# MoBA scores of the decoded samples on VectorE in place of TensorE, with their key pages spread over the attention stage

## The chip, the cores and the metric

The kernel runs on one core of a Trainium2 chip. A core has a matrix engine (TensorE, PE in the profile; its weight loads have a row of their own, PEld), a vector engine (VectorE, DVE), a scalar engine (ScalarE, ACT), a general one (GpSimd, POOL) and a queue that issues most transfers (SyncE, SP). Each runs its own list of instructions in order, and they wait for one another by semaphores. The metric is the time of one execution on the device in microseconds (us), as the median of several runs. About 0.3% (some 1.8 us) is what a measurement of this kernel can tell from no change.

## The reference, cut to what matters

One decoder layer is run for a prompt of 512 tokens and for 8 decoded samples of one token each. Two token mixers work side by side on the same input: a sparse attention with three branches (NSA), and MoBA, 8 heads of 64 channels over blocks of 256 keys. Each sample has 1024 past keys, in 8 pages of 128 keys, which a page table finds in a cache. What the change touches is the product of a sample's MoBA query with all its past keys:

```python
# qc (8 samples, 1, 8 heads, 64); kb: past keys by block of 256; kmean: mean key of each block
gs  = einsum('bqhd,bnhd->bqhn', qc, kmean)             # which 3 blocks count
sel = top_k(where(block < own, gs, -inf), 3)
s   = einsum('bqhd,bhqkld->bhqkl', qc, ksel) * 0.125 + bias
p   = masked_softmax(concat([s, s_own]))
out = einsum('bhqn,bhqnd->bqhd', p, vsel) + ...
```

The kernel makes all 1024 products of a head and sample once (64 rows of 1024 scores, with the mean score of a block for the choice), leaves out the blocks that weren't chosen, and multiplies by the values. Everything is in float32; the large products of the prompt take a float32 number apart into two parts of a faster format (high and remainder), and three matmuls on the parts make one product.

## The kernel before, in words

The weights come in 46 column blocks of 512 KB. A block is split into its two parts (high on ScalarE, remainder on VectorE or GpSimd by a written list, `HL_LO`, tile `hl`) and is multiplied with the input `hT` in 48 matmuls of 260 columns, into two banks `d`. These are the rows `d<-hTh,hl` and `d<-hTl,hl`, the bulk of the work. Between them run three other streams:

- **the compression** (`phi_pair`, `dec_cmp`; tiles `craw`, `u`, `pr`, `cvd`), in the first quarter;
- **the attention of the prompt** (`attend`, 24 jobs of 4 row blocks): scores into a bank `s` (`s<-kd,q`), bias and row minimum on VectorE (L1273, L1275), exponentials on ScalarE (L1278), a reciprocal on VectorE (L1279), the scaling on GpSimd (L1280), transposes into a bank `pt` (L355), a copy to SBUF (L1288, tiles `pp`), and the product with the values into a bank `o`;
- **the decoded samples** (`dec_a`, `dec_b`), which read pages through three buffers `cr` of 1 MB (tiles `raw`) and use the single bank `e`. Their order was: the pages `slck` and `wink` of NSA's keys, 16 tiles `mobk` of MoBA's keys, NSA's values, 16 tiles `mobv` of MoBA's values.

For MoBA's scores a key page lies with the channels on the 128 partitions. A tile `zm` holds each sample's query in a column of its own among zeros, and for each of the 16 tiles four matmuls of 512 columns (`e<-raw,zm`, 32 output rows each) add the page's scores into the bank, one quarter of the partitions for each pair of heads; after 8 tiles the bank is copied to half of `xm`.

What sets the order: `line_up` lays each engine's instructions out by a written table (`QUEUES`), and a second table (`SLOTS`) says which of its buffers a tile takes. No scheduler decides anything at run time; an instruction that waits holds up all that stand behind it on its engine. On SP a page load that waits for one of the three `cr` buffers holds up the weight loads behind it.

Of the kernel before, what the change touches and what calls it, by code (L numbers as in the profile page):

```python
# [18 lines left out]
T = 512  # L19
NS = 8  # L20
# [38 lines left out]
COPY_ENG = "daa"  # L59
# [15 lines left out]
for _name, _w in (("ident", 128), ("rowmask", 1), ("ones", 1), ("p16", 1),  # L75
# [20 lines left out]
    "kv.kl": "01",  # L96
# [14 lines left out]
    "de.cr": "01201201201201201201201202010120120120120120",  # L111
# [4 lines left out]
    "at.pp0": "012012012012012012012012",  # L116
# [6 lines left out]
    "fm.m": "0123456120",  # L123
# [13 lines left out]
702-704 659-664 705-710 677-682 750-755 690-695 756-761 720-722 539-541 711-719 542-550 723-743 768-785 762-767 786-797 804-815 798-803 816-821
829-840 883-894 841-846 895-900 847-849 901-906 919-924 683-685 850-852 907-912 859-861 686-687 913-918 688-689 950-955 862-870 956-961 925-930
871-873 853-858 874-876 822-824 877-879 931-936 880-882 825-826 944-949 962-967 827-828 974-979 968-973 980-1009 937-943 1022-1033 1040-1047 1034-1039
1048-1065 1010-1015 1072 1016-1021 1085 1066-1071 1073-1078 1110-1113 1092-1097 1079-1084 1126 1098-1103 1086-1091 1139 1104-1109 1120-1125 1114-1119  # L140
1225-1226 1211-1212 1133-1138 1127-1132 1146-1157 1140-1145 1174-1179 1241-1243 1170-1173 1233-1234 1158-1169 1180-1185 1187-1192 1255-1256 1244-1246
1186 1247-1248 1193-1198 1263-1264 1213-1218 1271-1272 1219-1224 1249-1254 1199-1210 1227-1232 1257-1262 1235-1240 1289-1290 1307-1308 1279-1288
1295-1300 1265-1270 1291-1294 1273-1278 1309-1314 1331-1332 1301-1302 1317-1318 1345-1350 1355-1360 1315-1316 1325-1330 1319-1324 1339-1344 1333-1338
1361-1362 1351-1354 1365-1370 1385-1390 1363-1364 1303-1306 1371-1374 1395-1402 1375-1376 1451-1456 1383-1384 1377-1382 1403-1408 1461-1466 1391-1394
1409-1410 1449-1450 1415-1420 1423-1428 1421-1422 1411-1414 1433-1438 1493-1498 1431-1432 1429-1430 1439-1444 1507-1512 1485-1490 1457-1460 1491-1492
1445-1448 1503-1506 1475-1478 1529-1534 1467-1468 1519-1520 1469-1474 1513-1518 1499-1502 1555-1560 1521-1526 1563-1568 1479-1484 1561-1562 1587-1592
1595-1600 1527-1528 1573-1578 1543-1554 1603-1608 1615-1616 1585-1586 1539-1542 1617-1622 1601-1602 1569-1572 1627-1632 1609-1614 1583-1584 1653-1658
1535-1538 1579-1582 1593-1594 1669-1674 1635-1640 1633-1634 1661-1666 1651-1652 1675-1680 1623-1626 1693-1696 1645-1650 1667-1668 1641-1644 1681-1688
1659-1660 1705-1710 1697-1704 1689-1692 1737-1744 1719-1722 1711-1718 1727-1732 1745-1750 1769-1770 1754-1755 1723-1726 1771-1776 1756-1761 1751-1752
1762-1767 1781-1786 1791-1792 1733-1736 1817-1822 1793-1798 1831-1836 1809-1811 1753 1803-1808 1823-1824 1768 1812-1814 1777-1780 1815-1816 1787-1790  # L150
1827-1830 1851-1854 1799-1802 1855-1856 1837-1842 1825-1826 1857-1862 1845-1850 1843-1844 1879-1884 1887-1892 1885-1886 1911-1916 1901-1906 1909-1910
1867-1878 1897-1900 1925-1928 1863-1866 1929-1930 1945-1950 1893-1896 1919-1924 1943-1944 1907-1908 1959-1964 1917-1918 1965-1968 1931-1936 1994-1999
# [192 lines left out]
def build(tc, A):  # L345
# [26 lines left out]
    with ExitStack() as es:  # L372
# [25 lines left out]
        def p_e():  # L398
            return bank("e", 1)
# [229 lines left out]
        def early_load(n):  # L629
# [4 lines left out]
            for hf in range(2):  # L634
                if n == "ks" and hf:
                    t = [kvp.tile([128, T], F32R, name="kl", tag="kl", bufs=2) for _ in range(2)]
# [1392 lines left out]
```

## Time and profile before

| | |
|---|---|
| median of 3 runs | 586.03 us (584.95 to 586.43) |
| the profiled execution | 584.64 us, its span 582.8 us |
| granted TensorE clock | 0.996 |
| moved by DMA | 124.83 MB, 214 GB/s on the mean |

The span is the time from the first to the last instruction on the core. The page's "busy" of an engine is the time in which at least one of its instructions ran. Matmuls overlap in the pipeline, so their mean duration is longer than the distance at which they follow each other; for a cost on PE the distance between the starts is read from the timeline. A group's row reads: line, engine, operation, output tile <- input tiles, shape, count | busy us, mean ns of one | idle time before, and what ended it.

### The profile page before, as it was taken

To read this page: it belongs to the slowest core of one execution; us is meant where nothing else is said; L and a number is where in the kernel's file an instruction comes from. 1 tells how busy PE (TensorE), PEld (TensorE's weight loads), DVE (VectorE), ACT (ScalarE), POOL (GpSimd) and SP (SyncE) were. 2 spreads that over 40 slices of the span, in tenths; PEclk is the share of its full clock that TensorE was granted. 3 is DMA by queue.
4 is the path that set the end of the run, shared out by engine and by line. 5 is a ranking of instruction groups with operands and counts; after the bars stand their busy time and mean duration, and the time that the engine had idled before them with its cause. 6 is when DMAs were issued, how large, how long until landed. Compare 5 with 4: busy or idle time off the path is not lost.

```text
span 582.8 us, 13120 instructions
## 1 busy us (share of the span) xinstructions
PE 567.0 (97%) x4672; PEld 491.8 (84%) x4672; DVE 306.3 (53%) x839; ACT 288.9 (50%) x681; POOL 278.5 (48%) x312
## 2 busy tenths in 40 slices
PE   6899999999899999999999999999999999999994
PEld 4699999999897887977779898997878688889774
DVE  2577445516575665554454364675441254655476
ACT  2468555635364756645534374575442442323352
POOL 0223477453354436244344754453560456666715
PEclk9999999999999999999999999999999999999998
DMA  8996666511654794298878478450989998352503
GB/s 313 405 355 210 198 195 204 173 49 58 206 153 116 251 330 141 91 310 280 299 247 304 155 272 262 136 185 31 357 258 322 367 333 270 105 180 77 193 31 147
DMA packets 63667, 124.83 MB, mean 214 GB/s; under 512 B 8114, under 2 KB 25970, under 8 KB 63090
## 3 DMA queue, kind: packets, MB, share of 16 engines
q1 hardware_dynamic: 62194, 119.80, 60.8%
q0 software_dynamic: 1408, 4.20, 2.2%
q8 instruction: 37, 0.61, 0.4%
q14 instruction: 28, 0.23, 0.1%
HBM read 114.38 MB, written 9.58 MB: 213 GB/s over the span
## 4 chain that ended last, share of the span: by engine, by line
PE 91%; DMA 5%; DVE 1%; SPq 1%; issue 0%; POOLq 0%; POOL 0%; ACT 0%; DVEq 0%
PE d L352 55%; PE s L352 13%; PE e L352 8%; PE o L352 7%; PE pt L355 5%; DMA u<-ada_ss 2%; PE pt L352 2%; DMA y<-ada_ss 2%; DMA raw<-mobv 1%; PE d L355 1%; PE e L355 1%; SPq L358 1%; DVE kd L367 0%; SPq L575 0%; DVE dn L1109 0%
## 5 line engine op out<-in xcount | busy, mean ns | idle before, releaser
L352 PE MATMUL d<-hTh,hl 128*128 128x260 f32 (+1 forms) x1392 | 264.9, 288 | 0.0
L352 PEld LDWEIGHTS d<-hTh,hl 128*128 128x128 f32 (+1 forms) x1392 | 215.3, 188 | 3.5 <-issue 2.1
L352 PE MATMUL d<-hTl,hl 128*128 128x260 f32 (+1 forms) x704 | 198.1, 282 | 0.0
L352 PEld LDWEIGHTS d<-hTl,hl 128*128 128x128 f32 (+1 forms) x704 | 131.7, 187 | 0.0
L367 POOL TENSOR_TENSOR hl<-raw,hl 128x512 fp32r<-128x512 f32 x56 | 74.3, 1328 | 103.1 <-ACT hl L449 79.5
L449 ACT CAST hl<-raw 128x512 fp32r<-128x512 f32 (+1 forms) x103 | 63.0, 617 | 41.3 <-PE d L352 22.9
L1278 ACT ACTIVATE p<-s,sm 128x384 f32<-128x384 f32 (+3 forms) x96 | 50.7, 530 | 58.9 <-DVE sm L1275 39.8
L1280 POOL TENSOR_SCALAR p<-p,sm,gp 128x128 f32<-128x128 f32 (+3 forms) x64 | 41.5, 657 | 67.0 <-DVE sm L1279 59.1
L367 DVE TENSOR_TENSOR hl<-raw,hl 128x512 fp32r<-128x512 f32 (+1 forms) x47 | 41.0, 871 | 16.5 <-ACT hl L449 16.1
L352 PE MATMUL d<-yh,hl 128*128 128x260 f32 x256 | 47.4, 285 | 0.0
L352 PEld LDWEIGHTS d<-yh,hl 128*128 128x128 f32 x256 | 40.2, 188 | 3.0 <-issue 2.1
L1288 ACT COPY pp<-pt 128x512 f32<-128x512 f32 (+1 forms) x48 | 23.0, 479 | 34.0 <-PE pt L355 33.8
L355 PE MATMUL pt<-first_in,p 128*128 128x128 f32 x240 | 39.3, 278 | 0.0
L355 PEld LDWEIGHTS pt<-first_in,p 128*128 128x128 f32 x240 | 27.2, 140 | 11.2 <-issue 4.0
L352 PE MATMUL d<-yl,hl 128*128 128x260 f32 x128 | 36.2, 283 | 0.0
L1275 DVE CUSTOM_DVE_ANT_0 s<-s,band 128x256 f32<-128x256 f32 (+1 forms) x48 | 17.2, 366 | 35.9 <-PE s L352 31.7
L1280 POOL TENSOR_SCALAR p<-p,sm,first_in 128x256 f32<-128x256 f32 (+3 forms) x32 | 21.5, 677 | 27.2 <-DVE sm L1279 23.6
L1273 DVE TENSOR_REDUCE sm<-s 128x1 f32<-128x128 f32 (+1 forms) x48 | 17.0, 354 | 27.9 <-PE s L352 27.4
L352 PE MATMUL s<-kd,q 128*128 128x256 f32 (+3 forms) x96 | 31.3, 329 | 0.0
L367 POOL TENSOR_TENSOR u<-craw,u 128x512 fp32r<-128x512 f32 x16 | 21.4, 1345 | 19.2 <-ACT u L1038 12.3
L352 PE MATMUL s<-kd,qx 128*128 128x256 f32 (+3 forms) x96 | 30.2, 321 | 0.0
L352 PE MATMUL s<-u,w1h 128*128 128x256 f32 (+1 forms) x128 | 28.7, 291 | 0.0
(415 smaller groups left out, 1046.7 us busy)
## 6 DMA issues: line engine op xcount, KB each, us to landing
raw<-w_cols SPq DMA_DIRECT2D x46, 512.0 KB, 6.2
raw<-mobk SPq DMA_DIRECT2D x64, 256.0 KB, 4.4
raw<-mobv SPq DMA_DIRECT2D x64, 256.0 KB, 4.4
craw<-cmp SPq DMA_DIRECT2D x64, 128.0 KB, 2.9
u<-ada_ss SPq DMA_DIRECT2D x12, 512.0 KB, 7.8
raw<-slck SPq DMA_DIRECT2D x64, 64.0 KB, 2.0
raw<-ada_g SPq DMA_DIRECT2D x8, 512.0 KB, 4.9
raw<-w_up SPq DMA_DIRECT2D x8, 512.0 KB, 6.6
```

Source lines behind the costliest of these rows:

```text
L352: return mmraw(out, lhsT, rhs, start=start, stop=stop, skip_group_check=True)
L355: return nc.tensor.transpose(out, x, unit)
L358: return nc.sync.dma_start(out, x)
L367: (nc.gpsimd if eng == "p" else nc.vector).tensor_sub(out, x, f32(hi))
L449: nc.scalar.copy(h, src)
L1273: nc.vector.tensor_reduce(sm[:, 0:1], s[:, :b], axis=AX, op=OP.min)
L1275: nc.vector.tensor_tensor_reduce(out=s[:, b:n], in0=s[:, b:n], in1=j.band[:, 256 - (n - b):], scale=1.0, scalar=top, op0=OP.add, op1=OP.mi ...
L1278: nc.scalar.activation(pr, s[:, :n], AF.Exp, scale=-1.0, bias=sm[:, 1:2], accum_out=sm[:, 2:3])
L1280: D.setdefault("pool", []).append(nc.gpsimd.tensor_scalar(pr, pr, sm[:, 3:4], j.gate(i), op0=OP.mult, op1=OP.mult))
L1288: j.copied[gi] = (nc.scalar.copy if COPY_ENG[gi] == "a" else nc.vector.tensor_copy)(t[:, :n], p[:, :n])
```

## The change

MoBA's scores are made on VectorE. A key page now lies in the cache with the keys on the partitions (128 keys, each 512 channels in a row), so a tile `raw` of four pages is 128 x 2048.

- `q_rows` transposes the queries of the 8 samples, high part and remainder, into 16 rows of 512 (four transposes, two copies), and `sel` is a matrix of ones and zeros that picks a sample.
- `scores_m(b)` spreads sample b's query over all 128 partitions with one matmul of 512 columns (`e<-qr,sel`), and, for each of two tiles and twice for each, multiplies 128 x 1024 numbers in place by that bank (VectorE) and sums each head's 64 channels (VectorE) into `sc`.
- At the end eight transposes turn `sc`, and two copies bring it to `xm`.
- The key pages of sample b are fetched, and `scores_m(b)` runs, between the other steps of `dec_a`, samples 0 and 1 first, in place of one run of 16 tiles.
- All 24 copies of the first group of transposes (`COPY_ENG`, 128 x 512, 4 transposes each) go to ScalarE instead of VectorE; their buffers `pp0` are two instead of three.
- The sums `pr` of the new keys' scores (`new_scores`) no longer take bank `e` by themselves: two ride with the product `gsum`, the third with `seln`.
- Some tiles move to other pools: `kl` to the pool of the start, four of the seven tiles `m` to the pool of the end.
- The tables `QUEUES` and `SLOTS` are written anew, for all engines. On PE single matmuls of two or three streams now alternate where whole groups of 6 stood before.

```diff
-COPY_ENG = "daa"
+COPY_ENG = "aaa"
-    "kv.kl": "01",
+    "start.kl": "01",
-    "at.pp0": "012012012012012012012012",
+    "at.pp0": "010101010101010101010101",
-    "fm.m": "0123456120",
+    "fm.m": "012120",
+    "fin.mm": "0123",
...
-            totals = [new_scores(c, pp) for c in range(2)]
+            prs = [new_scores(c, pp) for c in range(2)]
             yield 2
             p = p_e()
+            for c in range(2):
+                mm(p[:, 64 + c:65 + c], prs[c], ones, True, True)
             mm(p[:, :64], const("gsum"), xc, True, True)
+            nc.vector.tensor_add(snew[:, 0:2], p[:, 64:66], bdn[:, 128:129].to_broadcast([128, 2]))
...
-        C = Pages([page_item("slck", [(4 * q + b4) * 8 + hf * 4 for b4 in range(4)], 128)
-                   for hf in range(2) for q in range(2)]
-                  + [plain_item("wink", q) for q in range(2)]
-                  + [page_item("mobk", [b * 8 + hf * 4], 512) for hf in range(2) for b in range(NS)]
-                  + [i for q in range(2) for i in (slcv_item(2 * q), slcv_item(2 * q + 1), plain_item("winv", q))]
+        C = Pages(mobk(0) + mobk(1) + [slck(0, q) for q in range(2)] + mobk(2) + [slck(1, q) for q in range(2)]
+                  + [plain_item("wink", q) for q in range(2)] + mobk(3)
+                  + [slcv_item(0), slcv_item(1), plain_item("winv", 0)] + mobk(4) + mobk(5)
+                  + [slcv_item(2), slcv_item(3), plain_item("winv", 1)] + mobk(6) + mobk(7)
                   + [page_item("mobv", [4 * q * 8 + k], 512, 8) for q in range(2) for k in range(8)])
...
+        def q_rows():
+            qhl = de.tile([128, 4, 2 * NS], F32R, name="qhl")
+            nc.scalar.copy(qhl[:, :, :NS], y[:, 4:8, T:])
+            lo(qhl[:, :, NS:], y[:, 4:8, T:], qhl[:, :, :NS], "d")
+            p = p_e()
+            for t in range(4):
+                tr(p[:2 * NS, t * 128:t * 128 + 128], f32(qhl[:, t]), ident)
+            qr = de.tile([2 * NS, 512], F32R, name="qr")
+            nc.scalar.copy(qr, p[:2 * NS])
+            sel = de.tile([2 * NS, NS], F32R, name="sel")
+            nc.vector.tensor_add(sel, ident[:2 * NS, :NS], ident[:2 * NS, NS:2 * NS])
+            return sel, qr
...
+            def scores_m(b):
+                p = p_e()
+                mm(p, sel[:, b:b + 1].to_broadcast([2 * NS, 128]), qr, True, True)
+                for hf in range(2):
+                    raw = C.take()
+                    for k in range(0, 4, 2):
+                        x = raw[:, k * 512:k * 512 + 1024]
+                        x3 = x.rearrange("p (k c) -> p k c", k=2)
+                        nc.vector.tensor_mul(x3, x3, p[:, None, :].to_broadcast([128, 2, 512]))
+                        nc.vector.reduce_sum(view(sc, (hf * 4 + k) * 128 + 2 * b, [[32, 8], [1, 2]]),
+                                             x.rearrange("p (u g c) -> p u g c", g=2, c=64), axis=AX)
+                    yield from C.fetch(2000)
...
-            xm = D["xm"] = de.tile([128, 1034], F32, name="xm", tag="x")
-            for hf in range(2):
-                s = p_e()
-                for b in range(NS):
-                    raw = C.take().rearrange("p (k t c) -> p t k c", k=4, t=4)
-                    for t in range(4):
-                      mm(s[grp(t)].rearrange("p (k c) -> p k c", k=4), zm[:, t, b], raw[:, t], b == 0, b == NS - 1)
-                    if b == NS - 1:
-                        nc.scalar.copy(xm[:, hf * 512:hf * 512 + 512], s)
-                    yield from C.fetch(1600 if hf and b == NS - 1 else 850)
...
+                for b in range(4 + 2 * q, 6 + 2 * q):
+                    yield from scores_m(b)
+            xm = D["xm"] = de.tile([128, 1034], F32, name="xm", tag="x")
+            for hf in range(2):
+                s = p_e()
+                for k in range(4):
+                    tr(s[:, k * 128:k * 128 + 128], sc[:, hf * 4 + k], ident)
+                nc.scalar.copy(xm[:, hf * 512:hf * 512 + 512], s)
...
-    d["mobk"] = f(mo[:, :, 0].reshape(NPHYS, 128, 4, 128).transpose(0, 3, 2, 1).reshape(NPHYS, 128, 512))
+    d["mobk"] = f(mo[:, :, 0].reshape(NPHYS, 128, 512))
```

How the tables move instructions is seen at three places. In the rows below a line number is that of the kernel they come from (before: L352 matmuls, L355 transposes; changed: L398 and L401), then come operation, output <- inputs, and the output's shape, with a count where equal ones follow each other.

The first place is PE in the attention stage, where the first tiles of MoBA's keys were scored. Before:

```order
L355 MATMUL pt<-first_in,p 128x128 x4
L352 MATMUL s<-ck_87,q_3096 128x64
L352 MATMUL s<-ck_87,q_3500 128x64
L352 MATMUL e<-raw,zm 32x512 x12
L355 MATMUL pt<-first_in,p 128x128 x4
L352 MATMUL s<-kd,q_3500 128x384
L352 MATMUL s<-kd,qx 128x384
```

In the changed kernel, at about the same place (some 40% of the weight matmuls done), sample 3's query is spread:

```order
L398 MATMUL s<-kd,q_3014 128x128
L398 MATMUL d<-hTh,hl 128x260
L398 MATMUL s<-kd,qx 128x128
L398 MATMUL e<-qr,sel 128x512
L398 MATMUL s<-ck_87,q_3473 128x64
L398 MATMUL d<-hTh,hl 128x260
L398 MATMUL d<-hTl,hl 128x260
L401 MATMUL pt<-first_in,p 128x128
```

All seven blocks of `e<-raw,zm` (64 matmuls in the program) are gone; eight single matmuls `e<-qr,sel` and eight transposes of `sc` stand in the changed queue.

The second place is VectorE where samples 4 to 6 are scored in the changed kernel; L1316, L1318 and L1322 are the minimum, the bias step and the reciprocal of the prompt's softmax (L1273, L1275 and L1279 before), L1539 multiplies a page and L1540 sums it:

```order
L413 TENSOR_TENSOR hl<-raw,hl 128x512
L1322 RECIPROCAL sm<-sm 128x1
L1316 TENSOR_REDUCE sm<-s 128x1
L1318 ISA s,sm<-s,band,sm 128x256
L1318 ISA sm 128x1
L1539 TENSOR_TENSOR raw<-raw,e 128x1024
L1322 RECIPROCAL sm<-sm 128x1
L1539 TENSOR_TENSOR raw<-raw,e 128x1024
L1540 TENSOR_REDUCE sc<-raw 128x8x2 x2
L1539 TENSOR_TENSOR raw<-raw,e 128x1024
L1318 ISA s,sm<-s,band 128x256
L1318 ISA sm 128x1
```

None of the rows of L1539 and L1540 was there before; a step of a softmax, or the remainder of a weight tile (L413), now has up to five of them ahead of it.

The third place is PE at the end of the compression. Before, the two sums `pr` stand behind the product `cvd` and each takes the bank by itself:

```order
L352 MATMUL e<-cvd,u 128x128 x4
L352 MATMUL d<-hTh,hl 128x260 x2
L352 MATMUL d<-hTl,hl 128x260
L352 MATMUL d<-hTh,hl 128x260 x2
L352 MATMUL d<-hTl,hl 128x260
L352 MATMUL d<-hTh,hl 128x260 x2
L352 MATMUL d<-hTl,hl 128x260
L352 MATMUL d<-hTh,hl 128x260 x2
L352 MATMUL d<-hTl,hl 128x260
L352 MATMUL e<-first_in,pr 128x1
```

In the changed queue they stand ahead of it, the first at the head of these rows and the second beside the product with `gsum` (`e<-xc,cstd`):

```order
L398 MATMUL e<-first_in,pr 128x1
L398 MATMUL d<-hTh,hl 128x260 x2
L398 MATMUL d<-hTl,hl 128x260 x3
L398 MATMUL e<-first_in,pr 128x1
L398 MATMUL e<-xc,cstd 128x64
L398 MATMUL d<-hTh,hl 128x260 x5
L398 MATMUL d<-hTl,hl 128x260
L398 MATMUL d<-hTh,hl 128x260
L398 MATMUL d<-hTl,hl 128x260
L398 MATMUL d<-hTh,hl 128x260 x4
L401 MATMUL e<-first_in,xg 64x128
```

The bank `e` has two turns fewer there; behind `cvd`, where the sums stood, it gets two new ones for the queries (`e<-first_in,qhl` and the first `e<-qr,sel`).

More of the change, by code (lines that the diff above doesn't have):

```diff
@@ L137 @@
[L137 to L140, printed above, removed]
@@ L635, in early_load @@
                 if n == "ks" and hf:
-                    t = [kvp.tile([128, T], F32R, name="kl", tag="kl", bufs=2) for _ in range(2)]
+                    t = [st.tile([128, T], F32R, name="kl", tag="kl", bufs=2) for _ in range(2)]
                 else:
@@ L1286, in turn @@
                 tr(p[:, k * 128:k * 128 + 128], j.p[i][:, kb * 128:kb * 128 + 128], ident)
[L1287 removed]
+            t = j.pt[gi] = at.tile([128, n], F32, name="pp", tag=f"pp{gi}", bufs=2)
             j.copied[gi] = (nc.scalar.copy if COPY_ENG[gi] == "a" else nc.vector.tensor_copy)(t[:, :n], p[:, :n])
@@ L1422, in take, with slck, mobk @@
                 return self.tiles.pop(0)
-        C = Pages([page_item("slck", [(4 * q + b4) * 8 + hf * 4 for b4 in range(4)], 128)
-                   for hf in range(2) for q in range(2)]
-                  + [plain_item("wink", q) for q in range(2)]
-                  + [page_item("mobk", [b * 8 + hf * 4], 512) for hf in range(2) for b in range(NS)]
-                  + [i for q in range(2) for i in (slcv_item(2 * q), slcv_item(2 * q + 1), plain_item("winv", q))]
+        def slck(hf, q):
+            return page_item("slck", [(4 * q + b4) * 8 + hf * 4 for b4 in range(4)], 128)
+        def mobk(b):
+            return [page_item("mobk", [b * 8 + hf * 4], 512) for hf in range(2)]
+        C = Pages(mobk(0) + mobk(1) + [slck(0, q) for q in range(2)] + mobk(2) + [slck(1, q) for q in range(2)]
+                  + [plain_item("wink", q) for q in range(2)] + mobk(3)
+                  + [slcv_item(0), slcv_item(1), plain_item("winv", 0)] + mobk(4) + mobk(5)
+                  + [slcv_item(2), slcv_item(3), plain_item("winv", 1)] + mobk(6) + mobk(7)
                   + [page_item("mobv", [4 * q * 8 + k], 512, 8) for q in range(2) for k in range(8)])
@@ L1463, in dec_a @@
             yield from C.fetch(2600)
+            sel, qr = q_rows()
+            sc = de.tile([128, 8, 128], F32, name="sc", tag="zm")
+            nc.gpsimd.memset(sc, 0.0)
+            def scores_m(b):
[10 more added lines that the diff above has]
+                    yield from C.fetch(2000)
             xs = de.tile([128, 1034], F32, name="xs", tag="x")
+            yield from scores_m(0)
             for hf in range(2):
+                yield from scores_m(1 + hf)
                 s = p_e()
@@ L1492, in dec_a @@
             ds, dw = own_p(xs, 1024, "oneb"), own_p(xw, 512, "oneb")
-            zm = de.tile([128, 4, NS, 32], F32, name="zm", tag="zm")
-            nc.gpsimd.memset(zm, 0.0)
-            for g in range(2):
-                yield from paced(lambda: nc.vector.tensor_copy(view(zm[OWN[g]], g, [[NS * 32, 4], [34, NS]]), y[OWN[g], 4:8, T:]))
-            yield 300
             tps = yield from turn_p([xq[:, j] for j in range(8)])
```

264 lines of the change are left out of this document (154 added, 110 removed).

## The prediction

> **What bounds the kernel now.** I read the page first: the engines' shares, the slices, the chain that ended last.
>
> ```profile
> PE 567.0 (97%) x4672; PEld 491.8 (84%) x4672; DVE 306.3 (53%) x839; ACT 288.9 (50%) x681; POOL 278.5 (48%) x312
> ...
> PE   6899999999899999999999999999999999999994
> ...
> PE 91%; DMA 5%; DVE 1%; SPq 1%; issue 0%; POOLq 0%; POOL 0%; ACT 0%; DVEq 0%
> ```
>
> TensorE is busy in 97% of the span, in nearly every slice, and 91% of the chain is its work: no other engine sets the end for long. Overlapped matmuls could hide gaps, so I look at stages, and at the distance between matmuls.
>
> ```profile
> 140.00:360.00 220.00, 218.26 (x1906) 186.37 (x1905) 118.99 (x407) 118.40 (x309) 100.84 (x119) 1.00 0.68 226
> 360.00:465.00 105.00, 104.85 (x858) 87.36 (x860) 49.58 (x153) 50.97 (x134) 47.29 (x57) 1.00 0.69 233
> ...
> 245.79 2.78 PE L352 MATMUL e<-raw,zm 128*32 128x512 f32 x24
> 248.50 0.66 PE L355 MATMUL pt<-first_in,p 128*128 128x128 f32 x4
> 248.92 0.42 PE L352 MATMUL s<-kd,q 128*128 128x384 f32 x1
> ...
> 251.74 0.39 PE L352 MATMUL s<-kd,q 128*128 128x512 f32 x1
> 251.96 0.40 PE L352 MATMUL s<-kd,qx 128*128 128x512 f32 x1
> 252.20 0.40 PE L352 MATMUL d<-hTh,hl 128*128 128x260 f32 x2
> ```
>
> The windows give PE, PEld, DVE, ACT and POOL busy, then clock, DMA share and GB/s. From 140 to 360 us, where all that changes lies, PE idles 1.74 us of 220, and the timeline shows it going from one block to the next without a hole. Here a microsecond of PE work is a microsecond of the end. DVE is at 119.0 of 220, 54%, with much of its idle time spent waiting for PE.
>
> **What leaves PE.** The chain lists the blocks of `e<-raw,zm` by duration; the first of each size:
>
> ```profile
> 245.86 2.71 PE e L352 x24
> 258.96 1.85 PE e L352 x16
> 315.66 0.99 PE e L352 x8
> ...
> L352 PE MATMUL e<-raw,zm x128: 592/592/617, 245.8 to 316.1; 128*32 128x512 f32 x128
> ```
>
> The 128 records (two for each of 64 matmuls) are three blocks of 24, three of 16 and one of 8: 3 x 2.71 + 3 x 1.85 + 0.99 = 14.7 us. The 592 ns of one would give five times that, but four, with 32 output rows each, overlap almost wholly.
>
> **What comes to PE.** A matmul of 512 columns of the faster format follows the next at 0.22 to 0.24 us (251.74, 251.96, 252.20): eight spread queries are 1.9 us. Four transposes take 0.42 us (248.50 to 248.92): eight of `sc` and four of the queries are 1.3 us. Together 3.1, so PE's own work falls by 11.6 us. That single matmuls of several streams now alternate I cost at nothing: the matmuls of different banks above follow one another at the same distance, and the blocks that run four at once stay whole.
>
> **The sums `pr`.** The one hole of PE in this stage:
>
> ```profile
> 146.76 0.28 PE L352 MATMUL d<-hTl,hl 128*128 128x260 f32 x1
> ...
> 148.78 0.38 PE L352 MATMUL e<-first_in,pr 128*128 128x1 f32 x2 [1.74 <-DVE ocmp L1169]
> ```
>
> The sum waited for VectorE to copy `ocmp` out of the same bank. It now stands ahead, and -1.7 us goes. Between nothing and all of it, I take all: but the queries' transposes wait for that same copy, and what is late next there is the first spread matmul, behind a copy of ScalarE with only some 1 us of matmuls between. The bound from the other side is that the same 1.7 stays.
>
> The sum without new waits: 584.64 - 11.6 - 1.7 = **571.3** for the profiled execution (its span 582.8 and 1.8 around it).
>
> **What comes to VectorE.**
>
> ```profile
> L1565 DVE TENSOR_TENSOR xm<-xm,dm 128x1024 f32<-128x1024 f32 x1 | 1.2, 1221 | 0.0
> L1560 DVE TENSOR_REDUCE gsum<-xm 128x4 f32<-128x1024 f32 x1 | 1.2, 1200 | 0.0
> L1483 DVE TENSOR_TENSOR xw<-xw,e 128x512 f32<-128x512 f32 x1 | 0.7, 684 | 0.0
> L476 DVE TENSOR_TENSOR gwt<-raw,gb 128x512 f32<-128x512 f32 x8 | 8.7, 1086 | 0.1
> ...
> L1288 DVE COPY pp<-pt 128x512 f32<-128x512 f32 x24 | 16.5, 687 | 21.3 <-PE pt L355 21.3
> L1288 ACT COPY pp<-pt 128x512 f32<-128x512 f32 x24 | 14.1, 588 | 27.1 <-PE pt L355 27.0
> ...
> 140.00:360.00 220.00, 11.69 (x17) 15.30 (x32) 1.00 0.68 226
> ```
>
> No row multiplies 128 x 1024 by a bank. One operand in SBUF and one in bank `e` cost 684 ns for 512 columns, and 512 columns more cost 1221 - 684 = 537 at most, so 1221 ns. Lower I see nothing; the upper bound is the product `gwt`, with both operands in SBUF and GpSimd at work beside it, 1086 / 684 = 1.6 times as long, 1.9 us. I take 1221, from the row with a bank as operand. The sum over channels reads as much as `gsum`: 1200. So 32 x 1.221 + 32 x 1.200 = 77.5 us, 4.84 a tile.
>
> The Trainium skill ("SBUF — State Buffer", Who interferes with whom) says that a VectorE instruction takes the port that it shares with GpSimd only for a second input in SBUF or in its two-port modes, and that a sum over the free dimension never does on trn2. By it the new products stay at 1221, and GpSimd isn't slowed; the 684 against 1086 above agrees. By the other bound the products would cost 22 us more of VectorE.
>
> Off VectorE go 24 copies of 687 ns; the last row (L1288 alone, DVE then ACT) has 17 of them, 11.7 us, in this stage. ScalarE gets them at 588 ns, 10 us on 118.4 of 220: 62% of the shorter stage, hidden. VectorE there: 119.0 + 77.5 - 11.7 = 184.8 in 220 - 13.3 = 206.7 us, **89%**. That is an average; the order has samples 4 to 7 (8 tiles) spread where 1187 to 1434 of the 2,096 weight matmuls are done, and the transposes at 1515 to 1599. Before, that was about here:
>
> ```profile
> 280.00:322.00 42.00, 42.00 (x342) 33.88 (x342) 19.23 (x67) 21.03 (x58) 16.70 (x20) 1.00 0.81 281
> 322.00:360.00 38.00, 38.00 (x453) 34.05 (x452) 17.43 (x60) 20.63 (x52) 24.61 (x28) 1.00 0.64 226
> ...
> 30.00:60.00 30.00, 30.00 (x265) 28.55 (x265) 24.06 (x47) 23.43 (x47) 10.56 (x9) 1.00 0.79 266
> ```
>
> PE's 80 us lose 7.4 of `zm` (one 2.71, two 1.85, one 0.99) and gain 1: 73.6. VectorE: 36.7 + 8 x 4.84 - 4.3 (80 / 220 of the copies) = 71.1, **97%**. Any delay stays until the pages are through. Behind a page's instructions wait the softmax steps and the remainders of weights, and behind those the others:
>
> ```profile
> POOL p L1280 <- DVE sm L1279: 82.7, 32, 8.6
> POOL hl L367 <- ACT hl L449: 80.4, 35, 6.7
> ...
> ACT p L1278 <- DVE sm L1275: 39.8, 25, 4.3
> ...
> L355 PE MATMUL pt<-first_in,p x240: 270/272/332, 170.4 to 445.4; 128*128 128x128 f32 x120
> ```
>
> GpSimd and ScalarE already wait 82.7 and 39.8 us for VectorE's softmax steps, at no cost, because the transposes come a job later (24 jobs, whose transposes run from 170.4 to 445.4: 11.5 us for one). What VectorE delivers more than that late, PE waits for.
>
> For these waits the lower bound is nothing. The upper one: the fullest window of VectorE in this trace is 24.06 of 30 us, 80%; if it got no further, 71.1 would need 88.9 us, 15 more than PE's 73.6. That window was set by PE, though, so 80% is no ceiling, and the truth is nearer to nothing: I take 3 (VectorE at 93%), and 1 for the first spread matmul: **4 us**. Profiled 575.3; the median before lies 586.03 - 584.64 = 1.4 above its profiled execution, so **576.5**.
>
> **The rivals.**
>
> *PE keeps everything covered.* No new wait: 571.3 + 1.4 = 572.7. For it: PE had almost none before, with waits for VectorE up to 8.6 us. Against: 97%.
>
> *VectorE becomes the bound; slower.* From samples 4 to 7 on it does not pass 80%: 571.3 + 15 + 1.4 = 588, and up to 599 if in addition the 16 products there cost the upper bound (16 x 0.7 = 11 us). It decides from products of 1.4 us on (16 x 0.18 = 2.9 us, VectorE's 71.1 then over PE's 73.6), or from a busy share that stops at 80%. For it: rows of 5 page instructions in line are 6 us in which no softmax step runs. Against: the product's second operand is in a bank.
>
> *The page buffers hold up SP.*
>
> ```profile
> SPq L358 <- PE e L352: 68.5, 15, 16.5
> ...
> L358 SPq DMA_DIRECT2D raw<-slck x64: 332/333/1328, 140.7 to 195.1; - x64
> L358 SPq DMA_DIRECT2D raw<-mobk x64: 332/333/1602, 200.8 to 302.1; - x64
> ```
>
> Page loads waited for PE to free a buffer, 16.5 us at the longest, and the weights behind them with it. Now VectorE frees it, a tile's 4.84 us later or more. If that is over the look-ahead two or three times, PE waits for weights: 576.5 + 2 x 4.84 = 586, no change. Against: the key pages now come first in the stream, where `slck` stood, 60 us earlier, so the same bytes have 160 us and not 100.
>
> **How the numbers follow.** The forecast, 576.5 (572 to 581 for itself): 0.60. All covered, 572.7: 0.18. SP, 586: 0.10. VectorE the bound, 588 to 599: 0.12. By the kernel's 0.3%, faster is under 584.3, slower over 587.8. The first two and a part of SP's (0.04) are faster: 0.82; the rest of SP's and a little of the last: 0.07; slower: 0.11. The range for 8 in 10 goes from 570, 2.7 under the full sum, for the rewritten end of the kernel where PE idles 7.5 us (the window below), to 585, most of the way to SP's case.
>
> ```profile
> 465.00:583.00 118.00, 110.50 (x792) 93.31 (x784) 65.75 (x127) 42.40 (x78) 69.06 (x64) 0.98 0.49 169
> ```
>
> **What would show it.** `e<-raw,zm` gone and PE's busy time in the order of 555; products near 1.22 and sums near 1.20 us; VectorE at 65% of the span and over 85% between the first product and the transposes of `sc`; idle time of PE under 6 us there, released by `p` or `hl`; the hole at `pr` gone. Wrong: PE idle by over 10 us between samples 4 and 7, products over 1.5 us, or weights that PE waits for on a DMA.

## The result, and the profile after

The changed kernel takes **583.01 us** (median of 5 runs, 582.84 to 583.52); the kernel before, measured with it, 586.03 (584.95 to 586.76). The ratio is 0.995, with a 95% interval of 0.9935 to 0.9965: 3.0 us faster. The direction was forecast, and the time lies in the range of 570 to 585, but the change was forecast at -9.5 us and is a third of that. That 583.0 lies in the range is luck: the upper end was drawn for weights that come late behind the page buffers, and no such wait appears. The profiled execution has a span of 581.1 us, with 1.7 us around it.

The page's engines, slices and chain, as they were shown of before:

```profile
PE 566.7 (98%) x4564; PEld 495.2 (85%) x4564; DVE 362.9 (62%) x878; ACT 304.0 (52%) x707; POOL 280.7 (48%) x312
...
PE   7999999999999999999999999999999999999994
...
PE 90%; DMA 3%; DVE 2%; issue 1%; POOL 1%; ACT 1%; SPq 1%; POOLq 0%; DVEq 0%; ACTq 0%
```

The same stretch of windows as in the prediction, and the part of it from the 1187th to the 1515th weight matmul, where the last 16 products stand:

```profile
140.00:360.00 220.00, 219.50 (x1845) 193.73 (x1844) 174.83 (x446) 132.58 (x337) 103.19 (x122) 1.00 0.67 222
275.90:349.00 73.10, 73.10 (x628) 63.28 (x627) 59.13 (x133) 41.14 (x107) 35.55 (x44) 1.00 0.70 243
```

The groups of VectorE's new work:

```profile
L1540 DVE TENSOR_REDUCE sc<-raw 128x16 f32<-128x1024 f32 x32 | 38.3, 1209 | 0.1
L1539 DVE TENSOR_TENSOR raw<-raw,e 128x1024 f32<-128x1024 f32 x32 | 38.3, 1214 | 1.0 <-PE e L398 0.6 <-DMA raw<-mobk 0.4
```

All of `e<-raw,zm` has left, and VectorE's new instructions have the size that was forecast. Its load hasn't: it is busy for 79% of the stage (174.83 of 220 us) and 81% of the later part (59.13 of 73.10), where the forecast had 89% and 97%. In the 220 us of the stage TensorE idles 0.5 us. Yet TensorE is busy for 566.7 us, where it was 567.0. So the time did not go into idle waits. It is inside the busy rows, and the distances between the starts have to say where. Two places of the timeline stand out. The first is a spread matmul between weight matmuls:

```profile
157.32 0.28 PE L398 MATMUL d<-hTh,hl 128*128 128x260 f32 x1
157.54 0.50 PE L398 MATMUL e<-qr,sel 16*128 16x512 f32 x1
157.96 0.38 PE L398 MATMUL d<-hTh,hl 128*128 128x260 f32 x1
158.18 0.28 PE L398 MATMUL d<-hTl,hl 128*128 128x260 f32 x1
```

From 157.32 to 158.18 are 0.86 us. Two weight matmuls are 0.12 each (in the run `rows_sel` below, 157.45 to 157.57), so the spread matmul holds TensorE for 0.62 us, and not for the 0.22 to 0.24 of the forecast. Its shape says 16*128 where its neighbours say 128*128: the stationary operand has only 16 rows. Taken this way all eight hold it for 4.8 us.

The second is the product with the values. Before, all 16 records of a pair of jobs followed each other, in each of the 12 pairs; the first pair:

```profile
184.68 2.37 PE L352 MATMUL o<-pp,v 128*64 128x512 f32 x16
186.98 0.50 PE L352 MATMUL s<-kd,q 128*128 128x512 f32 x1
```

Now some pairs are cut:

```profile
191.72 3.23 PE L398 MATMUL o<-pp,v 128*64 128x512 f32 x18
194.88 0.33 PE L401 MATMUL pt<-first_in,p 128*128 128x128 f32 x1
```

The first 16 of these 18 records are one pair; the last two are a single matmul of the next pair, whose partner in the other half of the columns runs 20 us later. Summed over all records, the distances of `o<-pp,v` went from 27.3 to 30.8 us and those of `o<-pc` from 3.9 to 4.7.

### The profile page after: what moved, and what is told of

Same layout as the page of the kernel before. It is cut to its first block, busy times and chain, and to the rows that moved or that the text cites. A ratio compares the mean times of both kernels' runs of the same rounds, so it can differ in the third digit from the quotient of the medians.

```text
span 581.1 us, 12955 instructions
## 1 busy us (share of the span) xinstructions
PE 566.7 (98%) x4564; PEld 495.2 (85%) x4564; DVE 362.9 (62%) x878; ACT 304.0 (52%) x707; POOL 280.7 (48%) x312
## 4 chain that ended last, share of the span: by engine, by line
PE 90%; DMA 3%; DVE 2%; issue 1%; POOL 1%; ACT 1%; SPq 1%; POOLq 0%; DVEq 0%; ACTq 0%
PE d L398 54%; PE s L398 13%; PE o L398 8%; PE e L398 7%; PE pt L401 5%; PE pt L398 2%; DMA first_in<-first 1%; DMA raw<-mobk 1%; POOL hl L413 1%; DMA lns<-rows 1%; PE e L401 1%; DMA raw<-w_cols 1%; PE d L401 1%; DVE yl L413 0%; SPq L404 0%
## 5 line engine op out<-in xcount | busy, mean ns | idle before, releaser
L398 PE MATMUL d<-hTh,hl 128*128 128x260 f32 (+1 forms) x1392 | 274.4, 289 | 0.5 <-DVE hl L413 0.5
L398 PEld LDWEIGHTS d<-hTh,hl 128*128 128x128 f32 (+1 forms) x1392 | 217.0, 188 | 4.2 <-issue 1.8
L398 PE MATMUL d<-hTl,hl 128*128 128x260 f32 (+1 forms) x704 | 181.2, 286 | 0.0
L413 POOL TENSOR_TENSOR hl<-raw,hl 128x512 fp32r<-128x512 f32 x56 | 74.6, 1335 | 122.1 <-ACT hl L495 109.7
L398 PEld LDWEIGHTS d<-hTl,hl 128*128 128x128 f32 (+1 forms) x704 | 125.6, 187 | 1.5 <-issue 0.8
L1321 ACT ACTIVATE p<-s,sm 128x512 f32<-128x512 f32 (+3 forms) x96 | 50.7, 529 | 38.7 <-DVE sm L1318 28.3
L413 DVE TENSOR_TENSOR hl<-raw,hl 128x512 fp32r<-128x512 f32 (+1 forms) x47 | 41.3, 879 | 27.4 <-ACT hl L495 27.1
L1331 ACT COPY pp<-pt 128x512 f32<-128x512 f32 (+1 forms) x72 | 37.1, 515 | 29.7 <-PE pt L401 19.5
L398 PE MATMUL d<-yh,hl 128*128 128x260 f32 x256 | 50.3, 288 | 1.0 <-ACT m L904 1.0
L398 PEld LDWEIGHTS d<-yh,hl 128*128 128x128 f32 x256 | 40.6, 188 | 5.0 <-issue 1.7
L401 PE MATMUL pt<-first_in,p 128*128 128x128 f32 x240 | 41.7, 276 | 0.4 <-POOL p L1323 0.4
L1539 DVE TENSOR_TENSOR raw<-raw,e 128x1024 f32<-128x1024 f32 x32 | 38.3, 1214 | 1.0 <-PE e L398 0.6
L1540 DVE TENSOR_REDUCE sc<-raw 128x16 f32<-128x1024 f32 x32 | 38.3, 1209 | 0.1
L401 PEld LDWEIGHTS pt<-first_in,p 128*128 128x128 f32 x240 | 28.2, 140 | 10.3 <-issue 3.8
L1323 POOL TENSOR_SCALAR p<-p,sm,first_in 128x512 f32<-128x512 f32 (+3 forms) x32 | 20.8, 661 | 28.1 <-DVE sm L1322 18.9
L1318 DVE CUSTOM_DVE_ANT_0 s<-s,band 128x256 f32<-128x256 f32 (+1 forms) x48 | 17.4, 363 | 26.3 <-PE s L398 18.7
L398 PE MATMUL d<-yl,hl 128*128 128x260 f32 x128 | 33.3, 283 | 0.0
L398 PE MATMUL o<-pp,v 128*64 128x256 f32 (+3 forms) x192 | 33.2, 441 | 0.0
L413 POOL TENSOR_TENSOR u<-craw,u 128x512 fp32r<-128x512 f32 x16 | 21.8, 1371 | 19.1 <-ACT u L1086 17.0
L398 PE MATMUL s<-u,w1h 128*128 128x256 f32 (+1 forms) x128 | 30.4, 290 | 0.0
```

The costliest lines, as they stand in the source:

```text
L398: return mmraw(out, lhsT, rhs, start=start, stop=stop, skip_group_check=True)
L401: return nc.tensor.transpose(out, x, unit)
L413: (nc.gpsimd if eng == "p" else nc.vector).tensor_sub(out, x, f32(hi))
L1318: nc.vector.tensor_tensor_reduce(out=s[:, b:n], in0=s[:, b:n], in1=j.band[:, 256 - (n - b):], scale=1.0, scalar=top, op0=OP.add, op1=OP.mi ...
L1321: nc.scalar.activation(pr, s[:, :n], AF.Exp, scale=-1.0, bias=sm[:, 1:2], accum_out=sm[:, 2:3])
L1323: D.setdefault("pool", []).append(nc.gpsimd.tensor_scalar(pr, pr, sm[:, 3:4], j.gate(i), op0=OP.mult, op1=OP.mult))
```

## Three theories

**A**: the gain was lost on TensorE itself, in blocks that don't use the whole array: the 16-row spread matmuls, and the cut products with the values. **B**, the forecast's own: the pages delay the softmax steps on VectorE, and TensorE waits for them, unseen in its busy rows. **C**: the removed blocks were never worth their 14.7 us.

## Experiment: VectorE without the pages

```diff
-                        nc.vector.tensor_mul(x3, x3, p[:, None, :].to_broadcast([128, 2, 512]))
+                        nc.vector.tensor_mul(x3[:, :, :16], x3[:, :, :16], p[:, None, :16].to_broadcast([128, 2, 16]))
                         nc.vector.reduce_sum(view(sc, ...),
-                                             x.rearrange("p (u g c) -> p u g c", g=2, c=64), axis=AX)
+                                             x.rearrange("p (u g c) -> p u g c", g=2, c=64)[:, :, :, :4], axis=AX)
```

> Edit: VectorE's products multiply 32 numbers a row instead of 1024, and its sums read 64 instead of 1024, so that MoBA's scores of the samples are not computed; every instruction, transfer and wait stays. VectorE's 76.6 us of pages become about 6. Theory B: the waits behind the pages go, 579 (the 4 us of the forecast) to 572.7 (all of it). Theories A and C: the pages cost TensorE nothing, 583.0 within 0.5.

Measured: 582.59 us (582.29 to 583.39), ratio to before 0.9943 (0.9923 to 0.9963). The two groups:

```profile
L1540 DVE TENSOR_REDUCE sc<-raw 128x16 f32<-128x64 f32 x32 | 6.3, 209 | 0.1
L1539 DVE TENSOR_TENSOR raw<-raw,e 128x32 f32<-128x32 f32 x32 | 5.2, 182 | 5.7 <-DMA raw<-mobk 4.2 <-PE e L398 1.5
```

The window of the stage:

```profile
140.00:360.00 220.00, 219.53 (x1846) 193.79 (x1845) 113.32 (x448) 131.31 (x338) 102.46 (x122) 1.00 0.67 223
```

VectorE loses 65 us of work (76.6 less 11.5), 61.5 of them in this stage, and the end doesn't move (span 581.6 against 581.1). B falls: the end differs by 0.4 us in the medians, which is within the noise, so at this load the pages cost it next to nothing.

## Experiment: the blocks `e<-raw,zm` made narrow, in the kernel before

```diff
-                      mm(s[grp(t)].rearrange("p (k c) -> p k c", k=4), zm[:, t, b], raw[:, t], b == 0, b == NS - 1)
+                      mm(s[grp(t)].rearrange("p (k c) -> p k c", k=4)[:, :, :16 if b else 128], zm[:, t, b],
+                         raw[:, t, :, :16 if b else 128], b == 0, b == NS - 1)
```

> Edit, to the kernel before: 56 of its 64 matmuls e<-raw,zm take 64 columns instead of 512 (the first sample's 8 stay, so that the bank is written whole), so that 7/8 of MoBA's scores of the samples are not computed; nothing else changes. Theories A and B (the 14.7 us were on the path): 14.7 / 8 = 1.8 stay for the whole ones and 12.9 / 8 = 1.6 for the narrow ones, 11.3 us less, 574.7. Theory C: less than half of that, above 580.

Measured: 580.59 us (579.16 to 583.5), ratio 0.9923 (0.9895 to 0.995); the span of the profiled run is 577.3, 5.5 less than before. Half of the expected 11.3. The group in its two shapes:

```profile
L352 PE MATMUL e<-raw,zm 128*32 128x64 f32 x112 | 3.6, 225 | 1.8 <-DMA raw<-mobk 1.8
L352 PE MATMUL e<-raw,zm 128*32 128x512 f32 x16 | 2.1, 605 | 0.0
```

Three rows of TensorE's timeline in which it now waits:

```profile
248.62 0.63 PE L355 MATMUL pt<-first_in,p 128*128 128x128 f32 x4 [1.28 <-DVE pp L1288]
269.42 0.32 PE L352 MATMUL e<-raw,zm 128*32 128x64 f32 x8 [0.91 <-DMA raw<-mobk]
285.70 0.32 PE L352 MATMUL e<-raw,zm 128*32 128x64 f32 x8 [0.46 <-DMA raw<-mobk]
```

The window around them:

```profile
240.00:320.00 80.00, 76.39 (x691) 66.28 (x692) 41.34 (x147) 43.69 (x119) 34.87 (x43) 1.00 0.81 282
```

The group's busy time fell from 15.2 us in the kernel before to 5.7, so 9.5 us of TensorE's work went, not 11.3: 64 columns cost more than an eighth of 512. Of these 9.5, TensorE idles 3.6 between 240 and 320 us, where it idled nothing before. In the old order the next limits, the key pages' transfers and VectorE's copies `pp`, stand close behind TensorE. By the line that was drawn beforehand (above 580), 580.59 lies on C's side, if only just; the rows say more than that line. Both answers hold in part: the work was on the path, and more than half of what left it arrived at the end, but the old arrangement could not have delivered all. The changed kernel spreads the pages and moves those copies, and in its stage TensorE idles 0.5 us; there the distances between starts of `e<-raw,zm`, 14.7 us before, are gone, and other rows have grown. So C doesn't explain its loss.

## Experiment: spread matmuls with 128 rows

```diff
-            qhl = de.tile([128, 4, 2 * NS], F32R, name="qhl")
-            nc.scalar.copy(qhl[:, :, :NS], y[:, 4:8, T:])
-            lo(qhl[:, :, NS:], y[:, 4:8, T:], qhl[:, :, :NS], "d")
+            qhl = de.tile([128, 4, 128], F32R, name="qhl")
+            nc.scalar.copy(qhl, y[:, 4:8, T + NS - 128:])
+            lo(qhl[:, :, :NS], y[:, 4:8, T:], qhl[:, :, 128 - NS:], "d")
...
-            qr = de.tile([2 * NS, 512], F32R, name="qr")
-            nc.scalar.copy(qr, p[:2 * NS])
-            sel = de.tile([2 * NS, NS], F32R, name="sel")
-            nc.vector.tensor_add(sel, ident[:2 * NS, :NS], ident[:2 * NS, NS:2 * NS])
+            qr = de.tile([128, 512], F32R, name="qr")
+            nc.scalar.copy(qr, p)
+            sel = de.tile([128, NS], F32R, name="sel")
+            nc.vector.tensor_add(sel, ident[:, :NS], ident[:, 128 - NS:])
```

> Edit: the queries' rows are made 128 high instead of 16 (the tile qhl holds 120 other columns of the queries beside the 8 remainders, sel is zero for those rows), so that the spread matmul e<-qr,sel uses all 128 rows of the array; the numbers computed are the same. Theory A (the gain was lost on TensorE itself, in blocks that don't use the whole array: a spread matmul of 16 rows holds TensorE for 0.60 us and not 0.24, and products with values that were cut into pieces pay for each cut): the spread matmul follows its neighbours at 0.24 us, 8 x 0.36 = 2.9 us less, 580.1. Theory B (VectorE's 77 us of pages delay the softmax steps, and TensorE waits for them unseen in its busy rows): no change, 583.0. Theory C (the removed blocks e<-raw,zm were never worth 14.7 us): no change.

Measured: 585.18 us (583.27 to 586.71), ratio 0.9989 (0.9973 to 1.0005). Against all three expectations it is slower than the changed kernel. The timeline of VectorE and then of TensorE at the first spread matmul:

```profile
145.23 1.17 DVE L1519 TENSOR_TENSOR sel<-first_in 128x8 fp32r<-128x8 f32 x1 [1.53 <-PE e L398]
...
148.26 0.66 PE L401 MATMUL e<-first_in,qhl 128*128 128x128 f32 x4 [2.47 <-DVE ocmp L1216]
```

The taller `sel` waits for TensorE, and the copy `ocmp` that frees bank `e` stands behind it on VectorE. Counted over all matmuls of 260 columns, the 601st runs at 122.6 us in this run and at 122.2 in the changed kernel, the 781st at 157.0 and 152.7: 3.9 us late at one place. The wait is 2.47 of them. Right behind it the granted clock (the third figure from the end of the row below) was half for 3.4 us, and there weight matmuls follow at 0.22 us and not at 0.12. Half of 3.4 makes 1.7 us more by estimate, and what the first spread matmul saves goes off:

```profile
148.80:152.20 3.40, 3.40 (x18) 3.30 (x17) 2.18 (x3) 1.20 (x2) 2.22 (x3) 0.50 0.88 252
```

Up to the 1,621st the 4.3 us of distance fall to 1.8, a step of some 0.36 for each of the seven later spread matmuls. So this run loses by a wait of its own, with what the clock added, and says, in its steps, that the 16 rows do cost what A says. The next run takes the wait away.

## Experiment: the same, with `sel` made three places later on VectorE

The edit is in VectorE's table alone: the instruction that makes `sel` stands behind the copy `ocmp` instead of three places ahead of it (the expectation says two; it passes a step `band`, a remainder `hl` and `ocmp`).

> Edit: the spread matmuls with 128 rows as in the run full_rows, and on VectorE the operation that makes sel stands two places later, behind the copy ocmp. In full_rows it waited 1.53 us for TensorE and held up ocmp, so that TensorE idled 2.47 us before the queries' transposes: the 0.36 us that each later spread matmul saved were spent there. Theory A: without that hold-up full_rows's 582.7 us of span lose the 3.9 us by which it was late at that place, and 8 x 0.36 = 2.9 us of the kernel after are gained: 580.1. If the price of 16 rows is no more than a rearrangement of waits (the rival now): 583.0, as the kernel after.

Measured: 581.65 us (580.56 to 581.86), ratio 0.9917 (0.9895 to 0.994); span 578.8. The same place as the first one shown of the changed kernel:

```profile
157.11 0.28 PE L398 MATMUL d<-hTh,hl 128*128 128x260 f32 x1
157.23 0.39 PE L398 MATMUL e<-qr,sel 128*128 128x512 f32 x1
157.45 0.28 PE L398 MATMUL d<-hTh,hl 128*128 128x260 f32 x1
157.57 0.28 PE L398 MATMUL d<-hTl,hl 128*128 128x260 f32 x1
```

Now 0.46 us lie between the rows that were 0.86 apart, and the spread matmul takes 0.22. The same numbers go into the same bank; only the rows of the stationary operand have changed. Eight times 0.40 would be 3.2; the span fell by 2.3, and the medians by 1.4. The changed kernel wasn't measured again beside this run or the later ones; each has the kernel before beside it (586.07), and the ratios to that are compared. Here the two intervals overlap from 0.9935 to 0.994, so the size of the gain on the end is known to about 1 us, while the distance in the trace is plain.

The Trainium skill ("TensorEngine Tiling (Array Packing)", Tiling Modes, Key Properties) says that a change of the tiling mode drains TensorE. The trace fits this, since the distances just before and just behind the 16-row matmul grow as well (0.22 us each in place of 0.12); that a drain is what takes the time, no run here shows. The price is the trace's: a single visit of a 16-row matmul among full ones costs 0.40 us.

## Experiment: the products with the values put together

```diff
-    "at.pp0": "010101010101010101010101",
+    "at.pp0": "012012012012012012012012",
```

With it, seven moves in TensorE's table. A single matmul of 512 columns, or a piece of up to four, moves down to the rest of its pair, or one of 128 columns up. The copies `pp0` take three buffers again, since a cut pair frees a buffer early, and a joined one doesn't.

> Edit: the copies pp0 have three buffers as in the kernel before, and on TensorE the seven places where a pair's products with the values (o<-pp,v) stand in two pieces are put together, the earlier piece moved down to the later one or one matmul moved up; nothing else moves. Theory A: the rows o<-pp,v fall from 30.8 us (sum of the distances between starts) to the 27.2 of the kernel before, 3.6 us less, 579.4. Theories B and C: 583.0, or a little more since the moved pieces come later.

Measured: 583.17 us, ratio 0.9949 (0.9929 to 0.9969): no change. TensorE now idles where pieces were joined, as at these two places, for VectorE and for a page of MoBA's values:

```profile
296.26 0.53 PE L398 MATMUL s<-kd,q 128*128 128x256 f32 x2 [0.64 <-DVE c L1364]
...
451.56 1.36 PE L398 MATMUL e<-raw,tp 128*32 128x512 f32 x8 [2.16 <-DMA raw<-mobv]
```

The distances of `o<-pp,v` fell by 2.2 us and those of `o<-pc` by 0.8, and what they gave went into these waits and two smaller ones (0.68 and 0.41 us). Behind the wait of 2.16 us the granted clock was again half for 3.4 us (452.2 to 455.6), in an execution that took 584.88 us, 1.7 above the median of its runs.

## Experiment: five of the joins

The edit is the same, without the two pieces of two matmuls near which a wait appeared; and of the last piece, ahead of the pages `mobv`, only its lone matmul of 512 columns moves.

> Edit: as the run whole (three buffers pp0, pieces of o<-pp,v put together), but only at five of its places: not the two after which TensorE was seen to wait (0.8 us behind the values at 295 us, and 2.16 us for a page of MoBA's values at 451 us). Theory A: the joins at the five places save 0.3 to 0.9 us each as the trace of whole shows them, some 2.4 us: 580.6. Rival (a join only moves a wait): 583.0.

Measured: 580.17 us (579.81 to 581.53), ratio 0.9898 (0.9874 to 0.9921), span 578.6. The place where the changed kernel had 18 records:

```profile
191.63 2.38 PE L398 MATMUL o<-pp,v 128*64 128x512 f32 x16
193.93 0.33 PE L401 MATMUL pt<-first_in,p 128*128 128x128 f32 x1
```

From 191.63 to 193.93 are 2.30 us; before, 3.16 with two records more. The single matmul cost 0.86. At its new place, beside its partner, it costs nothing: from the first record of that pair to the transposes behind it (with products `o<-pc` and the block `e<-raw,zn` between) it is 5.01 us in the changed kernel and 5.02 here.

```profile
212.17 1.93 PE L398 MATMUL o<-pp,v 128*64 128x512 f32 x11
...
217.18 0.44 PE L401 MATMUL pt<-first_in,c 128*128 128x128 f32 x2
```

```profile
211.22 2.37 PE L398 MATMUL o<-pp,v 128*64 128x512 f32 x16
...
216.24 0.44 PE L401 MATMUL pt<-first_in,c 128*128 128x128 f32 x2
```

So a half-array matmul without its partner costs its whole length, and this part of A stands: five joins are worth 2.5 us of span, as expected, and the interval lies wholly below the changed kernel's. The third buffer of `pp0` belongs to the same edit and wasn't tried by itself.

## Experiment: both, and one step on ScalarE

TensorE idled at one more place of the changed kernel, for the evacuation `m` that stood on ScalarE behind a cast `yh`, which waited for VectorE:

```profile
473.61 0.51 PE L398 MATMUL d<-yh,hl 128*128 128x260 f32 x2 [0.98 <-ACT m L904]
...
473.05 0.22 ACT L1734 CAST yh<-y 128x40 fp32r<-128x40 f32 x1 [2.01 <-DVE y L1722]
473.18 0.38 ACT L904 ACTIVATE m<-d 128x260 f32<-128x260 f32 x1
```

The edit joins the runs `rows_sel` and `whole2` and exchanges these two instructions of ScalarE.

> Edit: rows_sel and whole2 together, and on ScalarE one evacuation m (L904) put ahead of the cast yh (L1734) that waits 2.01 us for VectorE, since TensorE idles 0.98 us for that evacuation at 472 us. Theory A: 583.0 - 2.9 - 2.4 - 1.1 = 576.6, which is about the time that was forecast for the change. Rival: 583.0 or a part of it.

Measured: **577.08 us** (576.55 to 579.04), ratio to before **0.9845** (0.9818 to 0.9873): 1.5% faster than the kernel before, three times the changed kernel's gain, and faster than both. The span is 576.6, 4.5 below the changed kernel's, where 2.3 + 2.5 + 1.1 would be 5.9. At the 2,040th weight matmul this run is 5.9 us ahead of the changed kernel, at the 2,220th 3.5 (and 1.0 comes back with `m`). Between the two it idles three times for a page, 1.5 us in all:

```profile
435.58 1.06 PE L398 MATMUL e<-raw,tp 128*32 128x512 f32 x8 [0.34 <-DMA raw<-mobv]
448.15 1.06 PE L398 MATMUL e<-raw,tp 128*32 128x512 f32 x8 [0.72 <-DMA raw<-mobv]
459.83 1.06 PE L398 MATMUL e<-raw,tp 128*32 128x512 f32 x8 [0.48 <-DMA raw<-mobv]
```

The windows ahead of this place:

```profile
380.00:400.00 20.00, 19.59 (x168) 17.56 (x167) 14.04 (x42) 13.52 (x37) 10.48 (x14) 1.00 0.27 83
400.00:420.00 20.00, 20.00 (x155) 14.81 (x156) 7.98 (x29) 10.98 (x28) 10.47 (x14) 1.00 0.96 347
```

The transfers are at 27% from 380 to 400 us and at 96% in the 20 us behind. Here stands the next limit: what TensorE saves earlier, it waits at MoBA's value pages. How much an earlier start of these loads would bring was not tried.

## Experiment: how much more VectorE can carry

```diff
-                                             x.rearrange("p (u g c) -> p u g c", g=2, c=64), axis=AX)
+                                             x.rearrange("p (u g c) -> p u g c", g=2, c=64)[:, :, :, None, :].to_broadcast([128, 8, 2, 2, 64]), axis=mybir.AxisListType.XY)
```

> Edit: VectorE's sums over the channels read each number twice (2048 numbers a row instead of 1024), so that MoBA's scores of the samples come out doubled; all else stays. VectorE gets some 32 x 1.2 = 38 us more. Forecast's way of counting (samples 4 to 7 have VectorE at 97% of TensorE's time already): 71.1 + 16 x 1.2 = 90.3 us against 73.6, so 17 us more there, 600. Theory A (VectorE has room, since the pages cost nothing): windows of 20 us show VectorE at 28 to 36 us of 40, so that 38 us more in 210 reach 97%: 583 to 590.

Measured: 602.45 us (600.07 to 606.52), ratio 1.0285 (1.0246 to 1.0325). The group of the sums, and two groups of TensorE that wait:

```profile
L1540 DVE TENSOR_REDUCE sc<-raw 128x16 f32<-128x2048 f32 x32 | 72.4, 2276 | 0.1
...
L398 PE MATMUL s<-kd,q 128*128 128x256 f32 x24 | 7.3, 305 | 3.4 <-DVE c L1366 2.6 <-ACT p L1321 0.8
L398 PE MATMUL e<-qr,sel 16*128 16x512 f32 x8 | 3.9, 494 | 2.4 <-DVE raw L1539 2.4
```

The window of the stage:

```profile
140.00:360.00 220.00, 208.47 (x1709) 180.55 (x1708) 188.60 (x414) 120.91 (x309) 93.72 (x112) 0.98 0.62 202
```

34.1 us more of sums cost 19.8 us of span (600.9 against 581.1). TensorE idles 11.5 of the 220 us, for VectorE and for steps of ScalarE that wait for it, and behind two of these waits (1.70 and 2.61 us) the granted clock was half for 3.4 us each. With the run without pages, this gives the shape of the curve: the first 65 us on VectorE were free, the next 34 cost more than half of themselves. Neither theory had this right. A's room of up to 97%, meant as a mean, is too much: VectorE is busy for 86% of these 220 us (188.60), though for 95% of single windows.

The forecast's counting gave 17 us for the stretch of samples 4 to 7, and that this is near 19.8 is luck: of the 19.8 us, 7.9 were lost ahead of that stretch and 1.4 behind it. The stretch itself, from the 1187th to the 1515th weight matmul, took 83.7 us where the changed kernel took 73.1. The first of these rows is that stretch, the second a window that VectorE fills to 95%:

```profile
283.70:367.40 83.70, 76.55 (x628) 64.14 (x627) 72.72 (x133) 41.35 (x107) 35.23 (x44) 0.98 0.64 213
260.00:300.00 40.00, 37.74 (x359) 32.45 (x358) 38.08 (x85) 22.07 (x59) 18.95 (x24) 1.00 0.73 236
```

VectorE's 72.7 us in it are the load that the forecast had expected of the change there (71.1). At that load the stretch grows by 10.6 us and not by 3; some 1.7 of them, by the estimate used above, are the halved clock.

## Why the prediction was right or wrong, point by point

- **What bounds the kernel.** Right. TensorE sets the end in this stage before and after, and every microsecond found later was found on it.
- **What leaves TensorE, 14.7 us.** The blocks are gone, as computed, and with them 14.7 us of distances. That such work was on the path is shown for the narrow blocks (9.5 us of work, 5.5 of the end, the rest in new waits of the old order).
- **What comes to TensorE, 3.1 us.** Wrong, and this is one of the two terms that failed. The transposes came at 1.0 us for the 1.3 forecast; the spread matmuls were priced from rows of 128*128; they are 16*128 and hold TensorE for 4.8 us in all, not 1.9. The runs with 128 rows show that the rows are the cause.
- **"Single matmuls of several streams ... alternate I cost at nothing ... the blocks that run four at once stay whole."** This is the other term that failed, by what it leaves out. Where a spread matmul of 128 rows stands among weight matmuls, in the run `rows_sel`, they keep their 0.12 us (157.11 to 157.23, 157.45 to 157.57), and it keeps its 0.22. Blocks that run four at once did not become dearer either: the distances of `e<-raw,tp` sum to 20.3 us before and 20.4 after. But the blocks of `o<-pp,v` run two at once, and several are cut; I had looked at the blocks of the pages alone. Their distances grew by 4.4 us with `o<-pc`; five joins gave 2.5 us of the end back.
- **The sums `pr`, -1.7.** Right; the queries' transposes that took their place at the copy of `ocmp` follow without a gap:

```profile
144.94 0.40 PE L398 MATMUL d<-hTh,hl 128*128 128x260 f32 x2
145.18 0.60 PE L401 MATMUL e<-first_in,qhl 128*16 128x128 f32 x4
145.53 0.48 PE L398 MATMUL d<-hTh,hl 128*128 128x260 f32 x2
```

- **What comes to VectorE, 77.5 us.** Right in size: 1214 and 1209 ns, against 1221 and 1200. The choice of the row with a bank as operand held, and so did the Trainium skill's rule on the shared port ("SBUF — State Buffer", Who interferes with whom) that was weighed there.
- **The shares of 89% and 97%.** Wrong: 79% and 81%. The new instructions are as long as forecast, so it is the work beside them that was counted too high. In the later stretch stand 16 products and 13 sums, 34.8 us where 38.7 were counted, and the rest of VectorE's work there is 24.3 us (59.1 less 34.8) where 32.4 were counted (36.7 less 4.3): the new tables put some of it elsewhere, the remainders `hl<-raw,hl` for one (4.8 us there, 6.7 before).
- **The waits, 4 us.** They aren't there at this load: without the pages the end is the same. TensorE's new idle times in the changed kernel are 0.5 us for a remainder at 169 us, 0.36 for a scaling at 363 and the 0.98 for `m`; the first and the last stand in the run without pages too. That the term was too large by only 2 us is in part luck, since two errors offset each other: the load was put too high, and the price at that load too low (10.6 us in the run with doubled sums, where 3 were forecast).
- **The rivals.** *PE keeps everything covered* is what VectorE did, but not its time. *VectorE becomes the bound* is a real mechanism that starts somewhere above this load (81% of the later stretch) and is there at the load of the last run (87%). *The page buffers hold up SP* doesn't show in the changed kernel; it shows for MoBA's values as soon as TensorE is faster.

The sum by measured terms: the forecast's span was 573.5 (575.3 less 1.8; its time should read 576.7 by its own terms, 575.3 + 1.4, not 576.5). The spread matmuls add 2.9, the cut products 4.4, and the waits are 1.9 in place of 4, so 2.1 less: 578.7. Of the 581.1, 2.4 us stay unassigned. Summed by rows, the distances of the weight matmuls (`d<-hTh,hl`, `d<-hTl,hl`, `d<-yh,hl`) grew by some 4.4 us outside the waits and the neighbours of the spread matmuls, and those of `pt<-first_in,p` by 1.2, while five rows of smaller products (`s<-ck,q`, `d<-ga,cst`, `s<-kd,q`, `pt<-w2hl,gl`, `d<-big,m`) fell by 3.3. So the rest lies among rows that now alternate, and the cost of alternating may be a little more than nothing; no run took it apart. Nor was the move of the copies to ScalarE undone by itself.

What the prediction had named as signs against it (idle TensorE, products over 1.5 us, late weights) did not happen: a loss inside the busy rows was not among them. Of its signs in favour, two failed and point at the two sides of the error: "PE's busy time in the order of 555" missed by 12, and VectorE "over 85%" between the first product and the transposes of `sc` was 80%.

## What to carry to other kernels

A matmul's price is read from a row of its own shape: before an edit moves or adds one that uses part of the array's rows or columns, look for what runs beside it, since a half-array matmul without its partner costs its whole length, and a 16-row one among full ones cost nearly three times a full one of the same columns. When an order table is rewritten, count the pieces of every block that runs several at once, of other streams too, and look at what buffer counts force cuts. And when an engine stays busy though work has left it, read distances between starts and add them up by shape; idle columns can't show such a loss.

## What the runs showed of the hardware that I had not expected

- A spread matmul of 512 columns between full matmuls: 0.62 us with a stationary operand of 16 rows, 0.22 with 128 rows.
- A matmul `o<-pp,v` of 64 output rows and 512 columns costs 0.86 us alone and nothing more beside its partner in the other half.
- Behind a wait of TensorE of 2.47 us (`full_rows`), 2.16 us (`whole`) and 2.61 us (`vector_double`) the granted clock was 0.50 for 3.4 us; in `full_rows` the weight matmuls followed at 0.22 us in it, in place of 0.12. It was so behind 1.70 us at 163 us of `vector_double` too, but not behind the 1.74 us of the kernel before; which waits bring it about, these runs don't show.
- VectorE's subtraction of 128x512 with both operands in SBUF takes 0.69 us, but 1.81 where a subtraction of GpSimd began 0.05 us before it (rows of the changed kernel's timeline below). It ends 0.56 us behind GpSimd's, so it looks like a wait for that end and not like a slower rate. The products with a bank as operand stay between 1203 and 1224 ns throughout. This is what the Trainium skill ("SBUF — State Buffer", Who interferes with whom) lets one expect of a second input in SBUF.

```profile
143.82 0.69 DVE L413 TENSOR_TENSOR hl<-raw,hl 128x512 fp32r<-128x512 f32 x1 [0.24 <-ACT hl L495]
167.90 1.81 DVE L413 TENSOR_TENSOR hl<-raw,hl 128x512 fp32r<-128x512 f32 x1 [0.71 <-ACT hl L495]
...
167.85 1.30 POOL L1273 TENSOR_TENSOR qx<-y,q 64x512 fp32r<-64x512 f32 x1
```
